# One transfer per query or key tile, bias tables kept on chip, and a moved logarithm in a two-layer attention trunk

## The chip, the cores and the metric

The kernel runs on one core of a Trainium2 chip. A core has TensorE (PE; its weight loads are shown as PEld), VectorE (DVE), ScalarE (ACT), GpSimd (POOL) and SyncE (SP), and 16 DMA engines that move data between the chip's memory (HBM, "DRAM" in the code) and the on-chip memory (SBUF). Nearly all transfers here are issued by SP, in the order of its own instruction queue. The metric is device microseconds of one execution, less is better.

## The reference, cut to what matters

The input is 2,048 tokens of 1,024 floats. Layer 0 has two attention mixers beside each other, layer 1 has one; each layer ends with a SiLU gate, an output projection and a residual add.

```python
# layer 0, mixer A: 8 query heads, 2 key heads, a window of own chunk and 2 before (chunks of 64), a learned sink
probs = softmax(concat([scores, sink]))[..., :-1]
# layer 0, mixer B: 8 heads, own chunk and 8 before, a learned bias by clipped distance
rel = clip(qpos[:, None] - kpos[None, :], -128, 128) + 128
scores = scores + rel_table[:, rel]
# layer 1: 8 heads, each with two maps (q1, k1) and (q2, k2) over all chunks up to the own one
a = softmax(s1) - lam * softmax(s2)
o = rms_norm(a @ v, subln_g) * (1.0 - lambda_init)      # the "sub-norm", per head
x = x + (o * silu(gate)) @ w_out
```

Queries and keys are RMS-normed per head (64 wide) before the scores; mixer A and layer 1 rotate them.

## The kernel before, in words

All arithmetic is in float32, with TensorE working on a high part (H, rounded to the matrix format) and a low part (L, the rest): one product is three or two matmuls. Each layer has a projection stage and a mixing stage. What the projection computes (queries, keys, values, gates) goes through scratch tensors in DRAM and is loaded again, tile by tile, by the mixing stage. Tokens go in 4 blocks of 512 (`BLK`), a block being 4 tiles of 128 (`P`).

*Scratch.* `scratch` (L103) makes one tensor per part: `akH`, `akL` (128 x 2048, two heads of 64 rows each), `bkH`, `bkL` for mixer B, and `qH`, `qL`, `kH`, `kL` (8 heads x 128 rows x 2048) for layer 1. The 128 rows of a layer 1 head are its two maps of 64 rows. `pairs_out` (L384) transposes normed queries or keys, splits them into `eH` and `eL` (three buffers each) and stores each with one transfer (L398, L399).

*Layer 0's mixing* (`_mix0`, L553). For every block from the last to the first, 16 heads alternate in pairs between A and B. `load_q` (L572) fills a query tile of 128 partitions in which the 64 rows of the head stand twice: two transfers for the high part (L577, L578) and two for the low part (L580, L581). `load_k` (L584) fills a key tile with high rows in partitions 0 to 63 and low rows in 64 to 127, again in two transfers (L587, L588). One matmul with the doubled queries then gives high x (high + low). For mixer B each head of each block also loads a bias table of 128 x 256 (L732), turns it round on POOL (L733) and sets a masked corner (L734). Query tiles have three buffers, key tiles, values and bias tables two.

`pace` (L49) lays out the order by hand: the heads' scores come first, the values of a head follow at a lag, and a side stream (late gates, then output projections of finished blocks) is put in between by the share of work done. The output weights' loads are a list; `next_load` (L838) takes one off it after each head (L859) and within the late gates (L866). The framework then orders the instructions of each engine by its own timing model, unless `tc.issue_after(x)` says that what follows is queued behind x on its engine.

*Layer 1's mixing* (`_mix1`, L893). The first two blocks are taken head by head, blocks 2 and 3 after that. `load_q` (L919) fills a tile of 128 partitions x 2 maps x 512 columns: for each part two transfers, one for each half of the partitions, each of 64 rows x 2 maps. `load_k` (L1088) fills a 128 x 512 key tile of one map in two transfers (L1093, L1094); for map 1 the low part stands in the lower half of the partitions. Key tiles have four buffers for each map, query tiles two. `scores` (L929) does the matmuls, a maximum on DVE (L955) and the exponential on ACT (L958), and remembers the newest one in `self.exp`. `gate` (L1030) is called when a head's values are done; its inner `rest` (L1042), called two key tiles into the next head's values, sums squares on PE (L1045), takes the logarithm on ACT (L1046), and goes on with an exponential and a product.

SBUF places are given pool by pool, in the order in which the pools are opened; the mixing stage's pools lie where the projection's pools lay and wait for what is still in use there.

Of the kernel before, what the change touches and what calls it, by code (L numbers as in the profile page):

```python
# [86 lines left out]
class Trunk:  # L87
# [15 lines left out]
    def scratch(self):  # L103
        dram = self.ctx.enter_context(self.tc.tile_pool(name="scr", bufs=1, space=DRAM))

        def d(name, shape):
            return dram.tile(shape, F32, tag=name, name=name)

        self.s0 = {
            "aqH": d("aqH", [4, P, S]), "aqL": d("aqL", [4, P, S]),  # L110
            "akH": d("akH", [1, P, S]), "akL": d("akL", [1, P, S]),
            "av": d("av", [S, 2 * 192]),
            "bqH": d("bqH", [4, P, S]), "bqL": d("bqL", [4, P, S]),
            "bkH": d("bkH", [4, P, S]), "bkL": d("bkL", [4, P, S]),
# [5 lines left out]
            "qH": d("qH", [8, P, S]), "qL": d("qL", [8, P, S]),  # L120
            "kH": d("kH", [8, P, S]), "kL": d("kL", [8, P, S]),
# [102 lines left out]
    def _project(self, es, layer):  # L224
# [15 lines left out]
        xp = pool("x", 3)  # L240
# [143 lines left out]
        def pairs_out(xs, npair, b, o):  # L384
            for p in range(npair):
# [12 lines left out]
                nc.sync.dma_start(s[o["dH"]][o["p0"] + p, :, b * BLK:(b + 1) * BLK], f32(eH))  # L398
                nc.sync.dma_start(s[o["dL"]][o["p0"] + p, :, b * BLK:(b + 1) * BLK], f32(eL))  # L399
# [153 lines left out]
    def _mix0(self, es):  # L553
# [3 lines left out]
        sm = pool("sm", 6)  # L557
        ld = pool("ld", 2)
        sb = pool("sb", 2)
# [12 lines left out]
        def load_q(H, L, h, b, res):  # L572
# [4 lines left out]
            nc.sync.dma_start(f32(qd[0:HD, :]), s[H][h // 2, r, tok])  # L577
            nc.sync.dma_start(f32(qd[HD:P, :]), s[H][h // 2, r, tok])  # L578
            ql = ld.tile([P, BLK], F32R, tag="ql", name=n + "ql", bufs=3)
            nc.sync.dma_start(f32(ql[0:HD, :]), s[L][h // 2, r, tok])  # L580
            nc.sync.dma_start(f32(ql[HD:P, :]), s[L][h // 2, r, tok])  # L581
            res["q"] = (qd, ql)

        def load_k(ks, H, L, p, row, k0, k1):  # L584

            r = slice(row * HD, (row + 1) * HD)
            nc.sync.dma_start(f32(ks[0:HD, :k1 - k0]), s[H][p, r, k0:k1])  # L587
            nc.sync.dma_start(f32(ks[HD:P, :k1 - k0]), s[L][p, r, k0:k1])  # L588
            return ks


        edge = ld.tile([P, 384], F32, tag="edge", name=n + "edge", bufs=1)
# [3 lines left out]
        win = ld.tile([P, 256], F32, tag="win", name=n + "win", bufs=1)  # L596
# [3 lines left out]
        nc.sync.dma_start(far, a["relfar"].to_broadcast([P, 8]))  # L600
        group = {}

        def load_group(b, g):
# [3 lines left out]
            load_k(ks, "akH", "akL", 0, g, k0, k1)  # L607
            vt = ld.tile([P, 5, 192], F32R, tag="vA", name=n + "vA", bufs=1)
# [19 lines left out]
        def join(yt, O, e):  # L628
            hi = slice(e * HD, (e + 1) * HD)
            lo = slice((1 - e) * HD, (2 - e) * HD)  # L630
            tmp = sb.tile([P, BLK], F32, tag="low", name=n + "low", bufs=1)
# [3 lines left out]
        def finish(yt, row, b):  # L635
            gt = ld.tile([P, BLK], F32, tag="gt", name=n + "gt", bufs=1)
# [201 lines left out]
        def next_load(upto=1):  # L838
            if loads and loads[0][0] <= upto:
                _, dst, src = loads.pop(0)  # L840
                nc.sync.dma_start(f32(dst), src)
                return True
# [521 lines left out]
```

## Time and profile before

| | us |
|---|---|
| median of three timed runs | 2790.53 (2790.26 to 2792.29) |
| the profiled execution, its own time | 2787.34 |
| its span, first to last instruction | 2785.4 |
| layer 0's projection, about | 0 to 601 |
| layer 0's mixing, about | 601 to 1126 |
| layer 1's projection, about | 1126 to 1734 |
| layer 1's mixing, about | 1734 to 2785 |

The profile is of one execution. Each engine has a busy time; the waits are named as "waiting instruction <- what released it: total, times, longest". The DMA view has one row for each group of transfers: destination and source, issuing queue, count, KB each, and the median time from issue to landing. The page says "packets" for the pieces that one DMA engine moves at a time: a row of a tile, mostly 2 KB. The granted clock of TensorE was 0.992 on average.

### The profile page before, as it was taken

Reading aid. Unit: us, or ns where it says so; the run is one execution under the profiler, and the core shown is the slowest. Engines: PE = TensorE matmul, PEld = TensorE weight load, DVE = VectorE, ACT = ScalarE, POOL = GpSimd, SP = SyncE. Lnnn points to the kernel's source line nnn. Section 1 sums busy time; section 2 is a strip of 40 time slices with the busy share of each in tenths; the row PEclk is TensorE's granted clock in tenths of the full one; section 3 lists DMA queues with packets and bytes.
Section 4 is the critical chain, followed back from the end, with each engine's and each line's share of the span. In section 5 each row is a group of like instructions: output and inputs, shape, how many; then the busy total and the mean of one; then the engine's idle time right before and its main releaser. Section 6 shows DMA issues by size and latency. Waiting matters only on the chain.

```text
span 2785.4 us, 43642 instructions
## 1 busy us (share of the span) xinstructions
PE 2687.8 (96%) x13384; PEld 2164.0 (78%) x13384; DVE 1814.8 (65%) x4520; ACT 1596.8 (57%) x3975; POOL 1425.9 (51%) x1519
## 2 busy tenths in 40 slices
PE   7999999999899999999999999999999999999999
PEld 6888887888788888788888888777777776676776
DVE  8662286336678776457844783478887787776772
ACT  5443544357777776333243332588887776676771
POOL 3641255235545454325554552467776666667661
PEclk9999999999999999999999999999999999999999
DMA  5674338739777665654386446899877666455542
GB/s 184 213 240 149 110 129 275 239 116 248 221 200 202 192 188 154 200 212 142 130 269 222 131 134 194 250 247 249 213 219 207 198 182 195 125 176 150 165 130 91
DMA packets 354041, 521.64 MB, mean 187 GB/s; under 512 B 42768, under 2 KB 137744, under 8 KB 353808
## 3 DMA queue, kind: packets, MB, share of 16 engines
q1 hardware_dynamic: 349200, 510.47, 61.0%
q10 hardware_dynamic: 4608, 8.39, 0.8%
q8 instruction: 107, 1.75, 0.3%
q14 instruction: 126, 1.03, 0.1%
HBM read 361.70 MB, written 157.02 MB: 186 GB/s over the span
## 4 chain that ended last, share of the span: by engine, by line
PE 68%; DMA 6%; DVE 3%; ACT 3%; issue 2%; POOL 1%; SPq 1%; ACTq 0%; DVEq 0%; POOLq 0%
PE cO L1010 8%; PE p1mm L216 6%; PE p1mm L215 6%; PE p1mm L214 6%; PE cS L951 4%; PE cS L952 4%; PE ctr L1006 4%; PE mom L214 2%; PE mom L215 2%; PE mom L216 2%; PE com L214 2%; PE cG L214 2%; PE com L215 2%; PE cG L215 2%; PE com L216 2%; PE cG L216 2%
## 5 line engine op out<-in xcount | busy, mean ns | idle before, releaser
L958 ACT ACTIVATE cP<-cS,cnm 128x512 f32<-128x512 f32 (+3 forms) x640 | 394.6, 623 | 137.9 <-DVE cnm L955 126.4
L955 DVE TENSOR_REDUCE cnm<-cS 128x1 f32<-128x512 f32 (+3 forms) x640 | 373.4, 600 | 53.8 <-PE cS L952 47.6
L992 POOL TENSOR_TENSOR cP<-cP,cP 128x512 f32<-128x512 f32 (+1 forms) x320 | 356.2, 1140 | 19.2 <-ACT cP L990 18.6
L991 POOL TENSOR_SCALAR cP<-cP,crl,cel 128x512 f32<-128x512 f32 (+3 forms) x288 | 208.8, 737 | 258.4 <-DVE crl L973 111.8
L216 PE MATMUL p1mm<-p1wH,p1hL 128*128 128x512 f32 x768 | 300.5, 392 | 0.0
L214 PE MATMUL p1mm<-p1wH,p1hH 128*128 128x512 f32 x768 | 300.2, 393 | 0.0
L215 PE MATMUL p1mm<-p1wL,p1hH 128*128 128x512 f32 x768 | 299.4, 390 | 0.0
L309 POOL TENSOR_TENSOR p0wL<-p0ws,p0wH 128x512 fp32r<-128x512 f32 (+1 forms) x140 | 169.9, 1240 | 251.0 <-ACT p0wH L307 232.4
L1010 PE MATMUL cO<-cpt,cv 128*128 128x512 f32 (+3 forms) x640 | 286.9, 534 | 5.6 <-DVE cpt L1008 5.6
L951 PE MATMUL cS<-ck,cqd 128*128 128x512 f32 (+3 forms) x640 | 260.6, 411 | 12.5 <-ACT cP L958 11.1
L1008 DVE COPY cpt<-ctr 128x512 f32<-128x512 f32 (+1 forms) x320 | 190.6, 604 | 101.0 <-PE ctr L1006 98.1
L214 PE MATMUL p0mm<-p0wH,p0hH 128*128 128x512 f32 (+1 forms) x640 | 239.1, 377 | 7.4 <-ACT p0vt L497 5.4
L216 PE MATMUL p0mm<-p0wH,p0hL 128*128 128x512 f32 (+1 forms) x640 | 239.3, 374 | 1.3 <-DVE p0hL L335 1.3
L215 PE MATMUL p0mm<-p0wL,p0hH 128*128 128x512 f32 (+1 forms) x640 | 239.5, 374 | 0.0
L952 PE MATMUL cS<-ck,cql 128*128 128x512 f32 (+3 forms) x640 | 233.1, 369 | 1.7 <-DMA cql<-qL 1.7
L1006 PEld LDWEIGHTS ctr<-ident,cP 128*128 128x128 f32 x1088 | 137.3, 141 | 120.0 <-issue 62.6
L309 POOL TENSOR_TENSOR p1wL<-p1ws,p1wH 128x512 fp32r<-128x512 f32 x112 | 154.3, 1402 | 138.8 <-ACT p1wH L307 80.6
L990 ACT ACTIVATE cP<-cP,cc 128x512 f32<-128x512 f32 (+1 forms) x320 | 188.9, 653 | 20.6 <-DVE cc L976 19.6
L1006 PE MATMUL ctr<-ident,cP 128*128 128x128 f32 x1088 | 174.8, 274 | 5.7 <-POOL cP L992 5.7
L216 PEld LDWEIGHTS p1mm<-p1wH,p1hL 128*128 128x128 f32 x768 | 144.2, 188 | 29.4
L215 PEld LDWEIGHTS p1mm<-p1wL,p1hH 128*128 128x128 f32 x768 | 144.3, 188 | 29.0
L214 PEld LDWEIGHTS p1mm<-p1wH,p1hH 128*128 128x128 f32 x768 | 144.3, 188 | 28.5
(320 smaller groups left out, 6937.3 us busy)
## 6 DMA issues: line engine op xcount, KB each, us to landing
p1ws<-in_od_w_in_dram SPq DMA_DIRECT2D x56, 512.0 KB, 3.7
p0ws<-in_ev_w_in_dram SPq DMA_DIRECT2D x48, 512.0 KB, 4.5
ck<-kH SPq DMA_DIRECT2D x144, 128.0 KB, 3.6
ck<-kL SPq DMA_DIRECT2D x144, 128.0 KB, 3.8
cv<-v SPq DMA_DIRECT2D x72, 256.0 KB, 4.4
cqd<-qH SPq DMA_DIRECT2D x64, 256.0 KB, 6.2
cql<-qL SPq DMA_DIRECT2D x64, 256.0 KB, 7.6
cwH<-wgH SPq DMA_DIRECT2D x64, 256.0 KB, 5.3
```

The lines of the kernel that those rows point to most:

```text
L214: mm(ps, aH, bH, start=first, stop=False)
L215: mm(ps, aH, bL, start=False, stop=False)
L216: mm(ps, aL, bH, start=False, stop=last)
L309: low.tensor_tensor(l[:, :width], ws[:, k, :width], f32(h[:, :width]), ALU.subtract)
L951: mm(ps, qd[:, m, js], kt[:, :wd], start=True, stop=False)
L952: self.anchor = mm(ps, ql[:, m, js], kt[:, :wd], start=False, stop=True).ins
L955: nc.vector.tensor_reduce(nm[:, m, z:z + 1], ps, AX.X, ALU.max, negate=True)
L958: exp = nc.scalar.activation(chunks[z][:, :wd], ps, AF.Exp, bias=nm[:, m, z:z + 1], accum_out=acc).ins
L991: nc.gpsimd.tensor_scalar(p1, p1, rl[:, 0:1], e1, ALU.mult, ALU.mult)
L992: nc.gpsimd.tensor_tensor(p1, p1, p2, ALU.add)
L1006: nc.tensor.transpose(turned[:, (j - j0) * P:(j - j0 + 1) * P], us[j][kt // 4][:, kk:kk + P], self.ident)
L1010: mm(O[:, j0 * P:], v, T[:, :wd], start=(kt == 0), stop=(kt == nkt - 1), skip_group_check=True)
```

## The change

- Scratch: high and low keys stand in one tensor (`ak`, `bk`, `ck`), one after the other. Layer 1's queries are laid out by head, row, block, map and column, so that a row's two maps for a block lie together.
- A key tile is loaded by one transfer in both layers, with high rows always in the upper half. A query tile's part is loaded by one transfer whose source is repeated twice. Layer 1's query store writes the two maps in the new order.
- All eight bias tables are loaded once at the start of layer 0's mixing, into a tile of their own, and turned round at their first use, in the last block.
- Pools are opened in another order and some tiles move to pools of their own; layer 1's projection gets four input buffers where it had three.
- Output weights of layer 0 are issued behind the newest query load, and are also taken off their list at every other step of an output tile.
- The sub-norm's logarithm is queued behind the newest exponential.

```diff
+        ak, bk, ck = d("ak", [1, 2, P, S]), d("bk", [4, 2, P, S]), d("ck", [8, 2, P, S])
...
-            "akH": d("akH", [1, P, S]), "akL": d("akL", [1, P, S]),
+            "ak": ak, "akH": ak[:, 0], "akL": ak[:, 1],
...
-            "bkH": d("bkH", [4, P, S]), "bkL": d("bkL", [4, P, S]),
+            "bk": bk, "bkH": bk[:, 0], "bkL": bk[:, 1],
...
-            "qH": d("qH", [8, P, S]), "qL": d("qL", [8, P, S]),
-            "kH": d("kH", [8, P, S]), "kL": d("kL", [8, P, S]),
+            "qH": d("qH", [8, HD, NB, 2, BLK]), "qL": d("qL", [8, HD, NB, 2, BLK]),
+            "k": ck, "kH": ck[:, 0], "kL": ck[:, 1],
@@ _project
-        xp = pool("x", 3)
+        xp = pool("x", 3 + layer)
@@ pairs_out
-                nc.sync.dma_start(s[o["dH"]][o["p0"] + p, :, b * BLK:(b + 1) * BLK], f32(eH))
-                nc.sync.dma_start(s[o["dL"]][o["p0"] + p, :, b * BLK:(b + 1) * BLK], f32(eL))
+                for part, t in (o["dH"], eH), (o["dL"], eL):
+                    to = s[part][o["p0"] + p]
+                    by_map = layer == 1 and o["tab"] == "q"
+                    to = to[:, b].rearrange("r m t -> m r t") if by_map else to[:, b * BLK:(b + 1) * BLK]
+                    nc.sync.dma_start(to, f32(t))
@@ _mix0
         sm = pool("sm", 6)
+        ep = pool("ep", 1)
+        sb = pool("sb", 2)
+        pa = pool("pa", 2)
+        lv = pool("lv", 2)
+        mk = pool("mk", 1)
         ld = pool("ld", 2)
-        sb = pool("sb", 2)
@@ load_q, load_k
-            nc.sync.dma_start(f32(qd[0:HD, :]), s[H][h // 2, r, tok])
-            nc.sync.dma_start(f32(qd[HD:P, :]), s[H][h // 2, r, tok])
             ql = ld.tile([P, BLK], F32R, tag="ql", name=n + "ql", bufs=3)
-            nc.sync.dma_start(f32(ql[0:HD, :]), s[L][h // 2, r, tok])
-            nc.sync.dma_start(f32(ql[HD:P, :]), s[L][h // 2, r, tok])
+            for q, part in (qd, H), (ql, L):
+                self.asked = nc.sync.dma_start(f32(q), s[part][h // 2, r, tok].unsqueeze(0).to_broadcast([2, HD, BLK])).ins
...
-        def load_k(ks, H, L, p, row, k0, k1):
+        def load_k(ks, K, p, row, k0, k1):
...
-            nc.sync.dma_start(f32(ks[0:HD, :k1 - k0]), s[H][p, r, k0:k1])
-            nc.sync.dma_start(f32(ks[HD:P, :k1 - k0]), s[L][p, r, k0:k1])
+            nc.sync.dma_start(f32(ks[:, :k1 - k0]), s[K][p, :, r, k0:k1])
@@ bias tables
+        biases = ld.tile([P, 8, 256], F32, tag="bias", name=n + "bias", bufs=1)
+        for h in range(8):
+            nc.sync.dma_start(biases[:, h, :], a["relb"][h])
...
-            bias = ld.tile([P, 256], F32, tag="bias", name=n + "bias")
-            nc.sync.dma_start(bias, a["relb"][h])
-            nc.gpsimd.tensor_scalar(bias, bias, -1.0, far[:, h:h + 1], ALU.mult, ALU.add)
-            nc.gpsimd.memset(bias[0:HD, 192:256], POS)
+            bias = biases[:, h, :]
+            if b == NB - 1:
+                nc.gpsimd.tensor_scalar(bias, bias, -1.0, far[:, h:h + 1], ALU.mult, ALU.add)
+                nc.gpsimd.memset(bias[0:HD, 192:256], POS)
@@ projected (layer 0)
-                yield from self.out_tile(
+                for i, u in enumerate(self.out_tile(
...
-                )
+                )):
+                    if i % 2:
+                        next_load()
+                    yield u
@@ next_load
-                nc.sync.dma_start(f32(dst), src)
+                with tc.issue_after(self.asked):
+                    nc.sync.dma_start(f32(dst), src)
@@ _mix1: load_q
-                both = s[part][h, :, tok].rearrange("(m r) t -> r m t", m=2)
-                for o in range(2):
-                    nc.sync.dma_start(f32(q[o * HD:(o + 1) * HD]), both)
+                both = s[part][h, :, b].rearrange("r m t -> r (m t)")
+                nc.sync.dma_start(f32(q).rearrange("p m t -> p (m t)"), both.unsqueeze(0).to_broadcast([2, HD, 2 * BLK]))
@@ gate, rest
-                nc.scalar.activation(sq, ms, AF.Ln, bias=self.eps, scale=1.0 / P)
+                with tc.issue_after(self.exp):
+                    nc.scalar.activation(sq, ms, AF.Ln, bias=self.eps, scale=1.0 / P)
@@ _mix1: load_k
-            r, o = slice(m * HD, (m + 1) * HD), slice((1 - m) * HD, (2 - m) * HD)
-            nc.sync.dma_start(f32(k[r, :]), s["kH"][h, r, tok])
-            self.loaded = nc.sync.dma_start(f32(k[o, :]), s["kL"][h, r, tok]).ins
+            self.loaded = nc.sync.dma_start(f32(k), s["k"][h, :, m * HD:(m + 1) * HD, tok]).ins
```

The lines left out rename pools: `low`, `gt`, `sg` move to `ep`; `edge`, `win` to `mk`; `vA`, `v` to `lv`; `PA` to `pa`; calls of `load_k` name the joint tensor.

More of the change, by code (lines that the diff above doesn't have):

```diff
@@ L595, in _mix0 @@
         nc.gpsimd.memset(edge[HD:P, 0:64], POS)
-        win = ld.tile([P, 256], F32, tag="win", name=n + "win", bufs=1)
+        win = mk.tile([P, 256], F32, tag="win", name=n + "win")
         nc.gpsimd.memset(win, 0.0)
@@ L606, in load_group @@
             ks = ld.tile([P, 640], F32R, tag="ksA", name=n + "ksA", bufs=1)
-            load_k(ks, "akH", "akL", 0, g, k0, k1)
-            vt = ld.tile([P, 5, 192], F32R, tag="vA", name=n + "vA", bufs=1)
+            load_k(ks, "ak", 0, g, k0, k1)
+            vt = lv.tile([P, 5, 192], F32R, tag="vA", name=n + "vA", bufs=1)
             nc.sync.dma_start(
@@ L630, in join @@
             lo = slice((1 - e) * HD, (2 - e) * HD)
-            tmp = sb.tile([P, BLK], F32, tag="low", name=n + "low", bufs=1)
+            tmp = ep.tile([P, BLK], F32, tag="low", name=n + "low")
             nc.scalar.activation(tmp[hi, :], O[lo, :], AF.Copy)
@@ L635, in finish @@
         def finish(yt, row, b):
-            gt = ld.tile([P, BLK], F32, tag="gt", name=n + "gt", bufs=1)
+            gt = ep.tile([P, BLK], F32, tag="gt", name=n + "gt")
             nc.sync.dma_start(gt, s["g"][row:row + P, b * BLK:(b + 1) * BLK])
@@ L654, in scores_a @@
             nm, l, es_, r = small("anm", 4), small("al", 4), small("aes", 4), small("ar", 4)
-            pt = sb.tile([P, NTB, 256], F32, tag="PA", name=n + "PA")
+            pt = pa.tile([P, NTB, 256], F32, tag="PA", name=n + "PA")
             lows = [P if b * NTB + j == 0 else 0 for j in range(NTB)]
@@ L724, in scores_b @@
             load_q("bqH", "bqL", h, b, res)
-            ks = load_k(ld.tile([P, 1024], F32R, tag="ks", name=n + "ks"), "bkH", "bkL", h // 2, h % 2, k0, k1)
-            vt = ld.tile([P, 8, P], F32R, tag="v", name=n + "vB")
+            ks = load_k(ld.tile([P, 1024], F32R, tag="ks", name=n + "ks"), "bk", h // 2, h % 2, k0, k1)
+            vt = lv.tile([P, 8, P], F32R, tag="v", name=n + "vB")
             nc.sync.dma_start(
@@ L818, in late_gate @@
                 yield 1
-            sg = sb.tile([P, BLK], F32, tag="sg", name=n + "sg", bufs=1)
+            sg = ep.tile([P, BLK], F32, tag="sg", name=n + "sg")
             gt = yp.tile([P, BLK], F32, tag="xr", name=n + "gt", bufs=2)
@@ L919, in load_q @@
         def load_q(h, b):
-            tok = slice(b * BLK, (b + 1) * BLK)
             qd = ld.tile([P, 2, BLK], F32R, tag="qd", name=n + "qd")
```

2 lines of the change are left out of this document (1 added, 1 removed).

## Prediction

> **What bounds the kernel now.** I read the page's first part first, then the busy time by stage, then the waits of PE on a transfer, then the DMA view of the whole run and of single stretches. All times are microseconds.
>
> ```profile
> span 2785.4 us, 43642 instructions
> PE 2687.8 (96%) x13384; PEld 2164.0 (78%) x13384; DVE 1814.8 (65%) x4520; ACT 1596.8 (57%) x3975; POOL 1425.9 (51%) x1519
> DMA packets 354041, 521.64 MB, mean 187 GB/s; under 512 B 42768, under 2 KB 137744, under 8 KB 353808
> ```
>
> TensorE is the bound: 97.6 us of the span are idle, and no other engine is above 65%. The first two rows below are the end of layer 0's projection, in which the first loads of layer 0's attention are already issued, and layer 1's projection. Then come the three stretches that matter here: layer 0's attention (from its first query load at 533 to its last loads at 1078), a stretch of layer 1's projection in which queries are stored, and layer 1's attention (1690 to 2661). Columns: time, length, five busy times with counts, granted clock, share of the 16 DMA engines, GB/s.
>
> ```profile
> 533.00:601.00 68.00, 68.00 (x301) 56.31 (x300) 8.80 (x13) 23.36 (x38) 16.09 (x20) 1.00 0.53 168
> ...
> 1126.00:1690.00 564.00, 561.27 (x2654) 467.90 (x2653) 359.86 (x597) 205.41 (x419) 275.47 (x207) 1.00 0.55 180
> ```
>
> ```profile
> 533.00:1078.00 545.00, 517.72 (x3138) 450.54 (x3137) 363.67 (x1216) 372.74 (x971) 254.62 (x383) 0.99 0.71 199
> 1690.00:2661.00 971.00, 940.73 (x4294) 696.57 (x4293) 703.63 (x1851) 705.64 (x1856) 615.30 (x660) 0.99 0.70 199
> ```
>
> ```profile
> 1254.00:1348.00 94.00, 94.00 (x449) 78.48 (x447) 74.03 (x120) 31.14 (x65) 53.37 (x40) 1.00 0.41 135
> ```
>
> In both attention stages the DMA engines are busy for seven tenths of the time on average, and PE still hardly waits for them. This is all of PE's idle time that ends with a query load:
>
> ```profile
> PE mSB L619 <- DMA mql<-bqL: 2.5, 4, 1.0
> PE mSA L619 <- DMA mql<-aqL: 2.4, 1, 2.4
> PE cS L952 <- DMA cql<-qL: 1.7, 2, 1.4
> PE cS L951 <- DMA cqd<-qH: 0.6, 1, 0.6
> ```
>
> 7.2 us, and no row names a key load. So what the change can win is small; what it can lose is the cover that the transfers have now, and that hangs on how many engines one transfer runs on.
>
> **How a transfer is divided now.** A quiet stretch shows it: from 300 to 320 only four gate tiles of 128 rows of 2 KB are stored.
>
> ```profile
> DMA packets 576, 1.05 MB, mean 52 GB/s; under 512 B 64, under 2 KB 64, under 8 KB 576
> q1 hardware_dynamic: 576, 1.05, 13.9%
> g<-p0gt SPq DMA_DIRECT2D x4, 256.0 KB, 2.4
> ```
>
> 512 packets are the rows; 64 small ones are left, sixteen for each transfer, one for each engine. 1.05 MB in 13.9% of 16 engines' 20 us is 23.6 GB/s for one engine. The same holds everywhere: the DMA view's 100 groups of issues, of which the first is p1ws x56, hold 2,057 transfers, and 2,057 x 16 = 32,912. The other 9,856 of the page's 42,768 small packets are the data rows under 512 B: cosines and sines 8,192, norms and lambdas 1,024, sinks and far bias 256, three gain columns 384. Even 256 bytes in 64 rows go to sixteen engines:
>
> ```profile
> p1ws<-in_od_w_in_dram SPq DMA_DIRECT2D x56, 512.0 KB, 3.7
> bq_g<-in_ev_b_q_norm_dram SPq DMA_DIRECT2D x2, 0.2 KB, 6.0
> ```
>
> So the division does not go by bytes. What all 2,057 share is an outermost loop over 64 or 128 rows. The change makes transfers with another outermost loop: a query load repeats its source twice (loop 2, zero step, over 64 rows), a key load takes high and low part (loop 2) over 64 rows, and layer 1's query store writes map by map (loop 2) over 64 rows. No row of before has an outermost loop of two. I bound such a transfer by sixteen engines (every row) and by two (one for each turn of the loop). I take two: rows of the outermost loop are the one unit that all transfers here have in common, and two turns give nothing to the other fourteen engines.
>
> The Trainium skill has a rule that speaks against this change. "DMA: Bandwidth & Descriptors", section "Rules for kernel authors", says that the engine count follows from the slowest loop of both sides, and that a leading zero-step broadcast of c copies holds the whole transfer to at most c engines. By it the sum is the one worked out below for two engines; the trace agrees in so far as loops of 64 and 128 run on sixteen, and it has no case of two.
>
> **The change, part by part.** These rows carry the bytes (KB each is 1,024 bytes; MB below is 10^6):
>
> ```profile
> mqd<-aqH SPq DMA_DIRECT2D x64, 128.0 KB, 4.2
> mql<-aqL SPq DMA_DIRECT2D x64, 128.0 KB, 4.5
> mqd<-bqH SPq DMA_DIRECT2D x64, 128.0 KB, 4.5
> mql<-bqL SPq DMA_DIRECT2D x64, 128.0 KB, 5.0
> mks<-bkH SPq DMA_DIRECT2D x24, 256.0 KB, 5.7
> mks<-bkL SPq DMA_DIRECT2D x24, 256.0 KB, 6.2
> mks<-bkH SPq DMA_DIRECT2D x8, 128.0 KB, 3.8
> mks<-bkL SPq DMA_DIRECT2D x8, 128.0 KB, 3.9
> mksA<-akH SPq DMA_DIRECT2D x6, 160.0 KB, 4.3
> mksA<-akL SPq DMA_DIRECT2D x6, 160.0 KB, 4.0
> ck<-kH SPq DMA_DIRECT2D x144, 128.0 KB, 3.6
> ck<-kL SPq DMA_DIRECT2D x144, 128.0 KB, 3.8
> cqd<-qH SPq DMA_DIRECT2D x64, 256.0 KB, 6.2
> cql<-qL SPq DMA_DIRECT2D x64, 256.0 KB, 7.6
> qH<-p1eH SPq DMA_DIRECT2D x32, 256.0 KB, 2.8
> qL<-p1eL SPq DMA_DIRECT2D x32, 256.0 KB, 3.2
> mbias<-in_relb_dram SPq DMA_DIRECT2D x32, 128.0 KB, 5.7
> ```
>
> And these what each of the three stretches moves in all, in the order 533 to 1078, 1254 to 1348, 1690 to 2661 (SP's queue, then ACT's queue in the last):
>
> ```profile
> q1 hardware_dynamic: 82669, 107.60, 70.4%
> ```
>
> ```profile
> q1 hardware_dynamic: 6784, 12.59, 41.0%
> ```
>
> ```profile
> q1 hardware_dynamic: 132632, 189.99, 68.9%
> q10 hardware_dynamic: 1152, 2.10, 0.6%
> ```
>
> The rate of one of the two engines is unknown: 23.6 GB/s from the quiet stretch above; 107.60 MB in 70.4% of 16 x 545 us is 17.5, and 189.99 MB in 68.9% of 16 x 971 is 17.7, when all sixteen pull at once. I take 22, near the quiet row, because fourteen engines would be nearly idle. Transfers on sixteen engines are issued on the same queue and close only when the two loaded engines have moved their rows too, so each stage needs the two engines' confined bytes plus one sixteenth of the rest.
>
> - *Layer 0's attention.* Queries 256 x 131,072 bytes = 33.6 MB, keys 12.6 + 2.1 + 2.0 = 16.7 MB, together 50.2. On two engines that is 25.1 MB each. The rest of the stage stays on sixteen: 107.6 less 50.2 less 24 bias tables (3.1) is 54.3, or 3.4 for each engine. 28.5 MB at 22 GB/s are 1,295 us where the stage has 545: **+750**.
> - *Layer 1's attention.* Queries 128 x 262,144 = 33.6 MB, keys 288 x 131,072 = 37.7; 71.3 MB make 35.65 for each of the two. The rest, 192.1 less 71.3, is 7.55 for each engine. 43.2 MB are 1,964 us instead of 971: **+993**. The cover is used up: PE has 940.73 us of work in this stage, so the transfers end last.
> - *Layer 1's query stores.* In the stretch of 94 us (the other half of the projection has one more, taken as equal) 32 stores of 262,144 bytes are 8.4 MB, 4.2 for each of two engines, and the rest of its 12.59 MB gives 0.26. 4.45 MB are 202 us. The three buffers of each part let six stores (36 us) trail; 202 - 94 - 36 = 72 stall the transposes that fill them, twice: **+144**.
> - *Bias tables.* 24 loads go; so do 24 of the rows below, off PE's path, and the 172.3 us of waiting cost no one but POOL, which works 254.62 of 545 us there. The eight loads now come in front of the first queries, behind 68 us in which PE still has layer 0's projection. 0.
>
> ```profile
> L733 POOL TENSOR_SCALAR mbias<-mbias,mfar 128x256 f32<-128x256 f32 x32 | 15.3, 479 | 172.3 <-DMA mbias<-in_relb_dram 172.3
> L1046 ACT ACTIVATE csq<-cms,eps 128x512 f32<-128x512 f32 x32 | 22.0, 687 | 46.8 <-PE cms L1045 46.8
> ```
>
> - *The sub-norm's logarithm* (L1046) keeps its 687 ns. Behind the newest exponential the 46.8 us that ACT stood at it can go to exponentials instead. Queued behind it are the exponential L1048 and the two-step output for the projection; that consumer runs a whole head later. Between -2 and +2; with ACT at 705.64 of 971 us, 0.
> - *Issue order and places.* Output weights are asked for behind the newest query load, the projection gets a fourth input tile, and pools lie elsewhere. PE's 561 of 564 us in that projection leave nothing to win. What they could cost is the second rival. 0.
>
> Sum: 750 + 993 + 144 = 1,887 us. The profiled execution took 2787.34 us (2 more than its span; 3.2 below the median of the three timed runs, which is about the 0.2%, 5.6 us, that a measurement can tell): 2,787 + 1,887 = **4,675 us** with two engines.
>
> **The rivals.** *All sixteen engines.* If the split reaches the 64 rows below the loop of two, each pair of loads becomes one and nothing is confined. Then the 7.2 us of query waits can go, nothing else on PE's path does: 2,780 us, faster by 0.26%. For it speaks that every transfer of before used sixteen; against it, that each had sixteen or more outermost rows. The Trainium skill's page named above, in the same section, advises one transfer of 128 partitions instead of two of disjoint halves; by that rule this rival's time is the result.
>
> *Sixteen engines and a late start.* Eight bias loads and the reordered places have to wait for memory of the projection; the first head's queries, behind them in SP's order, then come late. It decides once they are later than the 68 us that PE still works after 533. A table and a layer 0 query landing one after the other (5.7 + 5.0 us by their rows) leave PE idle for 10.7: 2,798 us, slower by 0.4%.
>
> *Only the repeated source is confined.* If zero-step loops are held to two engines but high and low parts are not, layer 0 has 33.6/2 + (107.6 - 33.6 - 3.1)/16 = 21.2 MB, 965 us (+420), layer 1 has 16.8 + 158.5/16 = 26.7 MB, 1,213 us (+242), and the stores cost nothing: 3,450 us.
>
> **How the numbers follow.** Two engines 0.83, sixteen 0.12, sixteen with a late start 0.02, only the repeated source 0.03. The weight of the first rests on the count of closing packets, which is blind to bytes, and on the loop of two that no transfer here has; the 0.12 on the possibility that the split sees through it. Within the first case, 23.6 GB/s gives +663, +860 and +124, 4,434 us; since that row is four transfers long I open it to 25 GB/s, 595 + 757 + 106, 4,245. The loaded rates give +1,084, +1,463 and +230, 5,564. The range 4,240 to 5,600 holds all but a few hundredths of the first case, 0.8 in all; what is left out are the three others. Faster: two thirds of the sixteen-engine case, 0.08; within 0.2%: 0.04; slower: 0.88.
>
> **What would show it.** If right, the small packets fall from 42,768 to 30,208 (848 transfers with 16 each go; 440 with two and eight bias loads with 16 come); at sixteen engines they would be 36,368. The mean share of the DMA engines drops in both attention stages while PE idles there, at about 57% of the span, with cqd, cql, ck, mqd, mql and mks as its releasers, and the granted clock falls in many slices; landing of these loads goes from 4 to 8 us to well above 10. The p1eH and p1eL copies wait for their stores. Wrong would be: landings under 8 us with PE still at 96% (sixteen engines), waits only for query loads (third rival), or PE idle at 533 to 620 alone (second).

## The result and the profile after

The changed kernel took 4579.18 us (median of five runs, 4575.36 to 4583.04) where the kernel before took 2792.29 beside it: ratio 1.6413, with a 95% interval of 1.6382 to 1.6443. It is 1,787 us slower. The forecast was 4,675.

The page of the changed kernel, the lines that answer to those shown of before, with the granted clock in 40 slices, SP's queue, and the chain that ended last by engine:

```profile
span 4574.7 us, 43129 instructions
PE 2998.7 (66%) x13384; PEld 2364.4 (52%) x13384; DVE 1810.2 (40%) x4520; ACT 1604.8 (35%) x3975; POOL 1404.5 (31%) x1471
PEclk9999976777777779978987877777777877788779
DMA packets 330214, 518.41 MB, mean 113 GB/s; under 512 B 30209, under 2 KB 122113, under 8 KB 329985
q1 hardware_dynamic: 325376, 507.27, 33.1%
DMA 47%; PE 29%; SPq 6%; DVE 3%; issue 3%; POOL 2%; ACT 1%; POOLq 0%; ACTq 0%; DVEq 0%
```

The granted clock and the chain of the kernel before:

```profile
PEclk9999999999999999999999999999999999999999
PE 68%; DMA 6%; DVE 3%; ACT 3%; issue 2%; POOL 1%; SPq 1%; ACTq 0%; DVEq 0%; POOLq 0%
```

Read the fourth line of the changed kernel first. 30,209 small packets: the prediction's count for two engines was 30,208, that for sixteen 36,368. The bytes are nearly what they were (518 MB against 522), the rate fell from 187 to 113 GB/s, and nearly half of the chain is DMA, which had 6% of it. PE's busy time grew by 311 us for the same 13,384 matmuls while the granted clock fell in most slices (mean 0.812, before 0.992); the other 1,478 us of the longer span are idle time of PE.

The waits of PE, the largest rows that end with a transfer (total, times, longest):

```profile
PE cS L962 <- DMA ck<-ck: 297.3, 64, 14.9
PE mSB L627 <- DMA mqd<-bqH: 166.9, 19, 16.1
PE mSB L628 <- DMA mql<-bqL: 130.4, 29, 6.0
PE cG L216 <- DMA cwH<-wgH: 119.3, 10, 20.5
PE cS L962 <- DMA cqd<-qH: 109.5, 7, 24.0
PE cS L963 <- DMA cql<-qL: 93.2, 10, 13.7
```

Five of the six are tiles that the change loads in one transfer. The sixth, cwH, is a gate weight whose transfer the change does not touch (3.0 us before): what is divided over sixteen engines is late too.

Where the time lies: three matmul groups of before, then of after, with the first and the last start (us) in the second half of each row. mSA and mtrB belong to layer 0's mixing, cS to the scores of layer 1.

```profile
L618 PE MATMUL mSA<-mksA,mqd x128: 219/283/386, 602.6 to 1074.2; 128*128 128x256 f32 x120, 128*128 128x128 f32 x8
L775 PE MATMUL mtrB<-ident,mPB x560: 270/273/435, 620.4 to 1116.5; 128*128 128x128 f32 x187
L951 PE MATMUL cS<-ck,cqd x640: 220/395/799, 1734.4 to 2706.5; 128*128 128x512 f32 x136, 128*128 128x128 f32 x8, 128*128 128x384 f32 x8, 128*128 128x256 f32 x8
```

```profile
L627 PE MATMUL mSA<-mksA,mqd x128: 220/415/582, 615.0 to 1710.0; 128*128 128x256 f32 x120, 128*128 128x128 f32 x8
L784 PE MATMUL mtrB<-ident,mPB x560: 270/273/436, 664.9 to 1778.0; 128*128 128x128 f32 x187
L962 PE MATMUL cS<-ck,cqd x640: 220/443/1041, 2618.4 to 4495.8; 128*128 128x512 f32 x136, 128*128 128x128 f32 x8, 128*128 128x384 f32 x8, 128*128 128x256 f32 x8
```

Up to the last mtrB after is 661.5 us later (1778.0 - 1116.5), from there to the first cS it loses 222.5 (840.4 instead of 617.9), between the first and the last cS 905.3 (1877.4 instead of 972.1), and behind that nothing (78.9 in both). Together 1,789, the whole difference of the spans. The forecast's terms for these parts were 750, 144 and 993.

The same by stage, in columns as in the prediction's rows (time, length, five busy times, clock, share of 16 engines, GB/s): layer 0's attention, one stretch of query stores, layer 1's attention.

```profile
533.00:1714.00 1181.00, 636.99 (x3120) 540.54 (x3118) 364.49 (x1213) 376.76 (x972) 239.52 (x337) 0.74 0.26 88
1912.00:2096.00 184.00, 110.40 (x451) 88.38 (x450) 74.56 (x122) 29.45 (x67) 51.97 (x40) 0.80 0.19 65
2574.00:4450.00 1876.00, 1064.98 (x4216) 762.64 (x4214) 695.20 (x1840) 718.26 (x1858) 619.41 (x665) 0.76 0.31 103
```

The share of the DMA engines fell from about 0.7 to 0.26 and 0.31 in the attention stages, although transfers now end last. That is how a few loaded engines look in a mean over sixteen. A stretch of 20 us in which queries are stored shows it bare, first by the DMA view, then by SP's timeline (start, length, instruction); the last fence is the start of the same stores, 112 us earlier:

```profile
DMA packets 508, 1.02 MB, mean 51 GB/s; under 512 B 8, under 2 KB 8, under 8 KB 508
q1 hardware_dynamic: 508, 1.02, 13.1%
```

```profile
2024.97 4.96 SPq L404 DMA_DIRECT2D qL<-p1eL  x1
2030.03 4.95 SPq L404 DMA_DIRECT2D qH<-p1eH  x1
2035.07 4.96 SPq L404 DMA_DIRECT2D qL<-p1eL  x1
2040.12 4.91 SPq L303 DMA_DIRECT2D p1ws<-in_od_w_in_dram  x1
```

```profile
1912.06 1.13 SPq L404 DMA_DIRECT2D qH<-p1eH  x2
1913.28 8.80 SPq L404 DMA_DIRECT2D qL<-p1eL  x2
```

13.1% of 16 is 2.1 engines (two packets are under way for 18 of the 20 us and three for the other 2); the four stores of the stretch closed with eight small packets, two each. The first two stores are handed over in 1.13 us together. After them each issue begins about 5 us behind the one before and lasts nearly as long: SP waits for room. That the room comes free as the two engines take a store in is inferred from these times. 131,072 bytes per engine in the 4.95 us of an issue are 26.5 GB/s, the rate that the sums below use; by the 5.05 us from one issue to the next it is 26.0. The weight load p1ws, which is divided over sixteen engines, stands in the same line.

### The profile page after: what moved, and what is told of

The parts are those of the page before. It is cut to its first block, busy times and chain, and to the rows that moved or that the text cites. A ratio compares the mean times of both kernels' runs of the same rounds, so it can differ in the third digit from the quotient of the medians.

```text
span 4574.7 us, 43129 instructions
## 1 busy us (share of the span) xinstructions
PE 2998.7 (66%) x13384; PEld 2364.4 (52%) x13384; DVE 1810.2 (40%) x4520; ACT 1604.8 (35%) x3975; POOL 1404.5 (31%) x1471
## 2 busy tenths in 40 slices
DMA packets 330214, 518.41 MB, mean 113 GB/s; under 512 B 30209, under 2 KB 122113, under 8 KB 329985
## 4 chain that ended last, share of the span: by engine, by line
DMA 47%; PE 29%; SPq 6%; DVE 3%; issue 3%; POOL 2%; ACT 1%; POOLq 0%; ACTq 0%; DVEq 0%
DMA ck<-ck 10%; DMA mql<-bqL 9%; DMA cql<-qL 5%; DMA cwH<-wgH 5%; DMA mql<-aqL 4%; PE cO L1021 4%; DMA qL<-p1eL 3%; PE cS L962 2%; DMA p1ws<-in_od_w_in_dram 2%; PE cS L963 2%; PE p1mm L218 2%; PE p1mm L216 2%; PE p1mm L217 2%; PE ctr L1017 2%; DMA x<-mxr 1%
## 5 line engine op out<-in xcount | busy, mean ns | idle before, releaser
L962 PE MATMUL cS<-ck,cqd 128*128 128x512 f32 (+3 forms) x640 | 293.2, 461 | 435.5 <-DMA ck<-ck 297.3
L962 PEld LDWEIGHTS cS<-ck,cqd 128*128 128x128 f32 x640 | 136.8, 214 | 493.9 <-issue 418.9
L217 PE MATMUL p1mm<-p1wL,p1hH 128*128 128x512 f32 x768 | 311.3, 405 | 47.1 <-POOL p1wL L311 47.0
L216 PE MATMUL p1mm<-p1wH,p1hH 128*128 128x512 f32 x768 | 312.3, 409 | 45.0 <-DVE p1xn L371 29.4
L963 PE MATMUL cS<-ck,cql 128*128 128x512 f32 (+3 forms) x640 | 260.3, 408 | 93.2 <-DMA cql<-qL 93.2
L218 PE MATMUL p1mm<-p1wH,p1hL 128*128 128x512 f32 x768 | 311.4, 406 | 0.0
L1021 PE MATMUL cO<-cpt,cv 128*128 128x512 f32 (+3 forms) x640 | 306.5, 567 | 0.6 <-DVE cpt L1019 0.5
L1017 PEld LDWEIGHTS ctr<-ident,cP 128*128 128x128 f32 x1088 | 147.0, 149 | 125.8 <-issue 70.7
L627 PE MATMUL mSB<-mks,mqd 128*128 128x384 f32 (+2 forms) x240 | 95.1, 397 | 177.9 <-DMA mqd<-bqH 166.9
L963 PEld LDWEIGHTS cS<-ck,cql 128*128 128x128 f32 x640 | 139.5, 218 | 114.2 <-DMA cql<-qL 96.7
```

The lines of the kernel that those rows point to most:

```text
L216: mm(ps, aH, bH, start=first, stop=False)
L217: mm(ps, aH, bL, start=False, stop=False)
L218: mm(ps, aL, bH, start=False, stop=last)
L962: mm(ps, qd[:, m, js], kt[:, :wd], start=True, stop=False)
L963: self.anchor = mm(ps, ql[:, m, js], kt[:, :wd], start=False, stop=True).ins
L1017: nc.tensor.transpose(turned[:, (j - j0) * P:(j - j0 + 1) * P], us[j][kt // 4][:, kk:kk + P], self.ident)
```

## The experiments

The theory: the outermost loop of a transfer sets how many engines it runs on, and the two loaded engines end last. Single runs stand beside 2789.17 (first four kernels), 2800.73 (next four) or 2788.15 (last four) of the kernel before on the same chip; 2800.73 is itself a single run, so differences from it are good to some 10 us.

**Rows outermost, and two transfers again.** If the loop order is the cause, the change loses nothing once each transfer has 64 or 128 rows outermost. The first kernel swaps the loops of every query and key load (rows then stand interleaved in partitions, in queries and keys alike, so the scores are the same); the second keeps everything else of the change but loads halves. Both send each of layer 1's query stores out as two transfers of 64 rows.

```diff
-  s[part][h // 2, r, tok].unsqueeze(0).to_broadcast([2, HD, BLK])
+  s[part][h // 2, r, tok].unsqueeze(1).to_broadcast([HD, 2, BLK])
...
-  nc.sync.dma_start(f32(ks[:, :k1 - k0]), s[K][p, :, r, k0:k1])
+  nc.sync.dma_start(f32(ks[:, :k1 - k0]), s[K][p, :, r, k0:k1].rearrange("i r t -> r i t"))
...
-  to = to[:, b].rearrange("r m t -> m r t") if by_map else to[:, b * BLK:(b + 1) * BLK]
-  nc.sync.dma_start(to, f32(t))
+  if by_map:
+      for m in range(2):
+          nc.sync.dma_start(to[:, b, m], f32(t[m * HD:(m + 1) * HD, :]))
```

> The changed kernel with one thing turned round: in every query and key load the loop over 64 rows is outermost and the loop of two (the repeat, or high and low part) is inside it, so that the row r stands in partitions 2r and 2r+1 of both tiles; the number of loads and their bytes stay. The query stores of layer 1, which cannot be turned, go out as two of 64 rows each. Theory (a transfer runs on as many engines as its outermost loop feeds, two in the changed kernel): all sixteen engines again, 2,770 to 2,795 us, PE busy about 96%, small packets 42,768 - 13,568 + 504 x 16 + 128 = 37,392. Rival one (a repeated source, a joint tensor or rows of 4 KB is slow as such): nothing changes but the stores, 4,350 to 4,600 us. Rival two (the stall comes from the bias loads, the places or the issue order): the same 4,350 to 4,600 us with the transfers quick and PE waiting for other things.

The second kernel loads each query and key tile in two transfers of 64 rows:

```diff
-  self.asked = nc.sync.dma_start(f32(q), s[part][h // 2, r, tok].unsqueeze(0).to_broadcast([2, HD, BLK])).ins
+  for o in range(2):
+      self.asked = nc.sync.dma_start(f32(q[o * HD:(o + 1) * HD, :]), s[part][h // 2, r, tok]).ins
```

> The changed kernel with every query and key tile loaded by two transfers of 64 rows, as before the change, and layer 1's query stores as two of 64 rows; bias tables on chip, places, issue order, the moved logarithm and the new layouts stay. Theory: 2,770 to 2,800 us. Against the kernel of before this is the worth of all parts but the single transfers, against the kernel with the row loop outermost it is the worth of the single transfers by themselves: I expect at most 10 us between the two, for a transfer less costs SP about half a microsecond that PE does not wait for. Rival two (the rest of the change makes the stall): over 4,000 us.

Measured: 2778.25 us with rows outermost (ratio to before 0.996, 0.9941 to 0.9979) and 2776.51 with two transfers (0.9954, 0.9939 to 0.997). The whole 1,787 us are gone in both. The page with rows outermost:

```profile
span 2772.8 us, 43210 instructions
DMA packets 337398, 518.44 MB, mean 187 GB/s; under 512 B 37392, under 2 KB 129296, under 8 KB 337168
```

The loads are as few as in the change and the bytes are the same; the closing packets rose from 30,209 to 37,392, sixteen for each transfer again. The outermost loop of two is the whole loss. That bias tables, places and issue order came along unchanged in both kernels clears them as well.

**Layer 1's keys alone.** The kernel before with one edit:

```diff
-  nc.sync.dma_start(f32(k[r, :]), s["kH"][h, r, tok])
-  self.loaded = nc.sync.dma_start(f32(k[o, :]), s["kL"][h, r, tok]).ins
+  self.loaded = nc.sync.dma_start(f32(k), s["k"][h, :, m * HD:(m + 1) * HD, tok]).ins
```

> The kernel of before with one part of the change: layer 1's key tiles come in one transfer whose outermost loop is of two. Theory: 37.75 MB on two engines is 18.9 each, the rest of the stage gives 154.3/16 = 9.6; 28.5 MB at the 26.5 GB/s that the changed kernel's back-to-back query stores show (131,072 bytes in 4.95 us) are 1,076 us where the stage has 971, and the two engines stood idle for a tenth of the time there, so 1,200: about 3,000 us (2,890 to 3,100), small packets 42,768 - 288 x 16 + 144 x 2 = 38,448. Rival (joint high and low parts are not confined, only a repeated source is): 2,780 to 2,795 us and 40,464 packets.

Measured: 3302.45 us, 513 more than before. That two engines carry it is right (38,448 small packets), so a loop over high and low part is confined just as a repeated source is, and the third rival of the prediction is out. The size missed: 513 where about 210 were expected.

**The query stores alone.** The new layout and the store map by map, with loads of two times 64 rows:

```diff
+  to = to[:, b].rearrange("r m t -> m r t") if by_map else to[:, b * BLK:(b + 1) * BLK]
+  nc.sync.dma_start(to, f32(t))
```

> The kernel of before with one part of the change: layer 1's queries in the new layout, each part stored by one transfer whose outermost loop is the two maps; loads stay two of 64 rows for each part. Theory: the two stretches of query stores take 184 us each as in the changed kernel, not 94: 2,787 + 180 = about 2,970 us (2,930 to 3,020), nothing lost in the attention stages. Rival (stores are not confined): 2,780 to 2,800 us.

Measured: 2994.98 us, 206 more than before, and 41,872 small packets. From this kernel's waits, four rows of one chain, then the wait that I had foreseen; below them the first row as it was before:

```profile
ACT p1wH L307 <- DMA p1ws<-in_od_w_in_dram: 140.3, 25, 21.3
POOL p1wL L309 <- ACT p1wH L307: 141.7, 25, 18.3
PE p1mm L215 <- POOL p1wL L309: 47.4, 6, 13.5
PE p1trq L388 <- POOL p1xn L381: 81.0, 10, 15.7
DVE p1eL L394 <- DMA qL<-p1eL: 151.6, 16, 14.2
```

```profile
ACT p1wH L307 <- DMA p1ws<-in_od_w_in_dram: 69.1, 27, 6.1
```

The copies do wait for their stores. But the projection's weights wait too: their loads are queued behind the stores on SP, and PE stands until they are split. PE's largest wait, 81.0 us that it did not have before, belongs to the same chain, as at 1297 us: POOL makes the normed queries p1xn in the order of its queue, and it stood 18.3 us before a weight split that comes ahead of them.

**Four turns instead of two.** The keys missed by so much that the count of engines had to be tested by itself. Keys are laid out in four groups of 32 rows, and the outermost loop has four turns:

```diff
+  ck = d("ck", [8, 2, 4, 33, S])
...
-  nc.sync.dma_start(f32(k[r, :]), s["kH"][h, r, tok])
-  self.loaded = nc.sync.dma_start(f32(k[o, :]), s["kL"][h, r, tok]).ins
+  self.loaded = nc.sync.dma_start(f32(k), s["k"][h, m, :, 0:32, tok]).ins
```

> The kernel before with layer 1's keys loaded in one transfer per tile whose outermost loop counts four (four groups of 32 rows, high and low) where the keys-alone kernel had two; each part of a key pair is stored in four transfers of 32 rows. Outermost loop sets the number of engines (my theory): four engines, 37.75 MB / 4 + 154.3 MB / 16 = 19.1 MB for each of them, 720 us at 26.5 GB/s where the stage has 971; the stage is nearly what it was, and the whole 2,790 to 2,900, the upper end for 192 more store issues in the projection. Rival (any loop outside the rows that is not itself the rows drops to the same slow path, whatever its count): about 3,300, as with two.

Measured: 3039.46 us, between the two. The page of this kernel:

```profile
DMA packets 353082, 521.65 MB, mean 172 GB/s; under 512 B 41808, under 2 KB 136784, under 8 KB 352848
```

42,768 - 288 x 16 + 144 x 4 + 192 x 16 = 41,808: four closing packets for each key load, sixteen for each of the 192 additional stores. Four turns run on four engines and cost 239 where two cost 513; the additional stores are in the 239. PE's wait for a key load, with two turns and then with four:

```profile
PE cS L953 <- DMA ck<-ck: 271.8, 59, 10.5
```

```profile
PE cS L959 <- DMA ck<-ck: 90.2, 33, 6.9
```

So the count matters and isn't a switch between one slow and one quick path. The loss was still far above what I expected for four.

**More key buffers.** One guess for the missing size was a ring: a key buffer comes free late, and its next tile then takes 5 us. Six buffers for each map, with room taken from the spare hidden tiles, and key loads that may run two tiles further ahead:

```diff
-  kp = pool("kp", 4)
+  kp = pool("kp", 6)
...
-  hx = pool("hx", 3)
+  hx = pool("hx", 1)
...
-  after, spare = [None, {}], NB - keys(b)
+  after, spare = [None, {}], NB + 2 - keys(b)
```

> The kernel before with layer 1's keys in one transfer of two outermost turns, as in the keys-alone kernel (3,302), but six key buffers for each map in place of four; room for them comes from two of three spare hidden tiles. Theory of a ring (two engines are only about 73% busy in that kernel's stage because a buffer comes free late and its next tile takes 5 us or more): 3,150 or less. Rival (the two engines' rate in this stage is simply lower, about 19 GB/s with the other traffic): unchanged, 3,260 to 3,320.

Measured: 3264.58 us, 38 less than with four buffers (one run each, on different chips), not the 150 that the ring asked for. PE's largest waits in this kernel:

```profile
PE com L216 <- DVE cxr L1184: 108.5, 5, 40.4
PE cG L216 <- DMA cwH<-wgH: 83.9, 10, 23.7
PE cS L953 <- DMA ck<-ck: 69.1, 10, 13.1
```

The wait for keys fell from 271.8 to 69.1 and came back at gate weights and at the residual (cxr), whose transfers are divided over sixteen engines. The ring is out as the main cause, and a throughput as what ends last fits: whoever asks next waits for it. What the two spare hidden tiles that were given up cost by themselves no run tells.

**Queries alone, and layer 0's keys alone.** Three kernels, each the kernel before with one group of loads in one transfer of two turns:

```diff
+  nc.sync.dma_start(f32(q), s[part][h // 2, r, tok].unsqueeze(0).to_broadcast([2, HD, BLK]))
```

> The kernel before with only layer 0's query parts loaded in one transfer, the source repeated twice outermost. My theory, two engines: 16.8 MB + 74.0 / 16 = 21.4 MB for each of the two, 808 us at 26.5 GB/s where the stage has 545: 3,050, and up to 3,130 if the two idle a fifth of the time. Rival (transfers one after the other, the two engines 73% busy as in the keys-alone kernel's stage): 1,107 us, 3,350. If a repeated source were not confined: 2,790.

```diff
+  nc.sync.dma_start(f32(q).rearrange("p m t -> p (m t)"), both.unsqueeze(0).to_broadcast([2, HD, 2 * BLK]))
```

> The kernel before with only layer 1's query parts loaded in one transfer, the source repeated twice outermost, and stored as two transfers of 64 rows in the new order. Two engines: 16.8 MB + 158.5 / 16 = 26.7 MB for each, 1,007 us at 26.5 GB/s where the stage has 971: 2,830, and up to 2,940 if keys queued behind a 10 us query transfer come late. Rival (73% busy): 1,380 us, 3,200.

```diff
+  nc.sync.dma_start(f32(ks[:, :k1 - k0]), s[K][p, :, r, k0:k1])
```

> The kernel before with only layer 0's key tiles loaded in one transfer of two outermost turns. If confined and divided transfers take turns (confined bytes at 26.5 GB/s on two engines, then the rest at 17.6 on sixteen, as the runs so far fit): 16.7 / 2 = 8.35 MB, 315 us, plus 90.9 / 16 = 5.7 MB, 323 us, and some 70 idle, 710 us where the stage has 545: 2,950. Rival (both kinds run beside each other and the two engines pull 26.5 GB/s throughout): 14.0 MB, 530 us, at most 2,840.

Measured: 3210.54 (+410), 3145.09 (+344) and 2967.59 (+179). The first two missed upward, as the keys had. The third was expected by another sum, 2,950, and came within 18.

That sum comes from the records of the DMA packets: for each moment of a stage, how many packets are under way. The number is near that of the engines at work, not the same: packets of one engine can overlap (before has up to 26 under way on sixteen engines, and the quiet stretch above three for a tenth of its time on two). Time in us by that number; the stretches are before's 533 to 1078 and 1690 to 2661, moved and lengthened by the shifts of mSA and cS in each kernel:

```
stretch                              0     1-2   3-4   5-8    9+   length
layer 0, before                     79      21    11    48   386      545
layer 0, queries alone              51     479   112    39   273      954
layer 0, keys alone                 49     233    52    64   328      726
layer 0, whole change               41     788   130    37   186    1,181
layer 1, before                    163      28    13    74   693      971
layer 1, keys, two turns           154     551   115    81   575    1,476
layer 1, keys, four turns          170      38   229   159   609    1,205
layer 1, queries alone              82     477    90   118   560    1,327
layer 1, whole change               87   1,095   173   100   420    1,876
```

Two engines work by themselves for most of what a stage has grown by, and with four turns the time moves from the column 1-2 to 3-4. So the two engines need their confined bytes at 26.5 GB/s and on top the time that their share of the divided packets takes now (before: 70.4% of 545 for 107.6 MB, 69.5% of 971 for 192.1 MB); then there is the time in which no engine works. With the column 0 read from each kernel, so that the sum is an account and not a forecast:

```
stretch                       confined/2   at 26.5   rest   none     sum   measured
layer 0, queries alone          16.8 MB       634     264     51     949        954
layer 0, keys alone              8.35         315     324     49     688        726
layer 0, whole change           25.1          947     194     41   1,182      1,181
layer 1, queries alone          16.8          634     557     82   1,273      1,327
layer 1, keys, two turns        18.9          712     543    154   1,409      1,476
layer 1, whole change           35.65       1,345     424     87   1,856      1,876
```

All six lie within about 5%, and still do at 26.0 GB/s. With four turns the same sum gives 356 + 543 + 170 = 1,069 against 1,205; that gap isn't explained. The kernel with six key buffers, counted alike, has 107 us without a packet where four buffers had 154, and 524 with one or two where they had 551: the buffers took idle time away, not the time of the two engines.

**Another issuing queue.** Is it SP's line that holds the divided transfers up? Layer 1's queries alone, issued by ScalarE:

```diff
-  nc.sync.dma_start(f32(q).rearrange("p m t -> p (m t)"), both.unsqueeze(0).to_broadcast([2, HD, 2 * BLK]))
+  nc.scalar.dma_start(f32(q).rearrange("p m t -> p (m t)"), both.unsqueeze(0).to_broadcast([2, HD, 2 * BLK]))
```

> The kernel with only layer 1's query parts in one doubled transfer (3,145), but these transfers issued on ScalarE's queue in place of SyncE's. If SyncE's queue is what makes divided transfers wait (nothing behind a confined transfer is issued while it is being issued), divided transfers now run beside the confined ones: the time in which only one or two DMA engines work falls from 459 us in the attention stage to under 200, and the whole to 2,830 to 3,000; ScalarE, with 705 us of work in a stage of 971, pays for its own issues of 5 to 10 us each. Rival (the DMA engines themselves take the two kinds in turns, whoever issues): 3,100 to 3,200 and the 459 us stay.

Measured: 3193.26 us, no better than from SP (3145.09), and the time with one or two packets under way was 526 us where it had been 477 by the table. In this kernel, an issue row of ScalarE and one of SP (minimum, median, maximum ns) and three waits of PE; below them two of these waits with the queries issued by SP:

```profile
L931 ACTq DMA_DIRECT2D cql<-qL x32: 489/490/9527, 1717.5 to 3008.1; - x32
L1098 SPq DMA_DIRECT2D ck<-kH x144: 444/516/1628, 1694.0 to 3065.5; - x144
PE cS L957 <- DMA cql<-qL: 109.0, 14, 13.5
PE cS L956 <- DMA ck<-kL: 53.2, 21, 8.6
PE cG L214 <- DMA cwH<-wgH: 14.8, 4, 5.3
```

```profile
PE cG L214 <- DMA cwH<-wgH: 95.5, 9, 19.1
PE cS L956 <- DMA ck<-kL: 1.8, 1, 1.8
```

ScalarE's issues mostly took half a microsecond, so it hardly paid. SP was no longer held: its longest issue of a high key part took 1.6 us, where one had taken 11.1 us with the queries on SP. Yet the divided key loads, which no longer stood behind confined ones on SP, were waited for 21 times instead of once; the wait for gate weights fell in turn. So here SP's line decided who waited and not how long the whole took, which leaves the engines themselves as the place where the transfers meet. The Trainium skill says so in "DMA: Bandwidth & Descriptors", section "Issuing engines are not separate DMA queues": whoever issues, transfers run on the same sixteen engines and interleave. The trace agrees.

**The two small edits alone.** The bias tables, then the logarithm, each put into the kernel before:

```diff
+  biases = ld.tile([P, 8, 256], F32, tag="bias", name=n + "bias", bufs=1)
+  for h in range(8):
+      nc.sync.dma_start(biases[:, h, :], a["relb"][h])
```

> The kernel before with only the bias tables loaded once and kept on chip. The change with every loop repaired gained 11 to 13 us (ratio 0.995 to 0.996). If the tables are what gained it: 2,775 to 2,780. My prediction's term for them (nothing): 2,785 to 2,791, ratio within 0.998 to 1.002.

```diff
-  nc.scalar.activation(sq, ms, AF.Ln, bias=self.eps, scale=1.0 / P)
+  with tc.issue_after(self.exp):
+      nc.scalar.activation(sq, ms, AF.Ln, bias=self.eps, scale=1.0 / P)
```

> The kernel before with only the sub-norm's logarithm queued behind the newest exponential. My prediction's term (between -2 and +2 us): ratio 0.999 to 1.001. If this edit is what the repaired change gained: 2,775 to 2,780, ratio 0.995 to 0.996.

Measured: tables 2780.84 us, ratio 0.9971 (0.9955 to 0.9987); logarithm 2791.35, ratio 1.0009 (0.9994 to 1.0025). The tables gain some 7 or 8 us, the logarithm nothing that can be measured. By the middle values the tables are most of the 11 to 13 us that the two repaired kernels gain; the intervals overlap, so that no further gain is shown.

## Why the prediction was right, and where its sizes were off

*Two engines.* Right, and shown: 30,209 closing packets, 2.1 engines busy in the quiet stretch, and the loss gone when only the loops are swapped. The step that carried it was the count of small packets: it told from the profile of before that each transfer closes on sixteen engines whatever its bytes, and so that the loops, not the bytes, decide. The Trainium skill's page "DMA: Bandwidth & Descriptors" agrees in its section "Rules for kernel authors"; the other rule of that section, one transfer of 128 partitions instead of two halves, holds only together with it: with rows outermost one transfer and two take the same time here (ratios 0.996 and 0.9954), with the loop of two outermost it costs 64%.

*The rate of 22 GB/s.* The mis-sized term, in both directions. A confined engine runs faster than I took (26.0 GB/s by SP's spacing of 5.05 us, 26.5 by the length of an issue), the divided bytes fit at the price that they had before (17.5 and 17.7), and the engines also stand idle for some time. Over a whole stage these make 28.5 MB / 1,181 = 24.1 GB/s in layer 0 and 43.2 / 1,876 = 23.0 in layer 1, close to 22; so +750 came out as +661 (with the tail of mtrB) and +993 as +905. That one rate for both kinds comes so close is luck: in the whole change the errors nearly cancel. Taken part by part the single rate is worse: layer 1's keys alone would have been 28.5 / 22 = 1,295 us, measured 1,476. The sum that fits prices the confined bytes and the rest apart. Layer 0's keys also lack two rows, mksA x2 of 128 KB for the high and the low part: 0.5 MB, or some 10 us of the +750 at 22 GB/s, and less than 10 us in the sums above.

*The stores.* +144, measured +206 alone and +222 in the change. The step that failed is the 36 us that six stores were to trail without harm. Bytes at 26.5 GB/s give 4.45 MB / 26.5 = 168 us, and the stretch took 184 (the second one, 2300 to 2484, too): nothing trailed, because the projection's weight loads stand behind the stores and are wanted at once. That +144 came near is again two errors, a rate too low and a trail that isn't there. Two stretches lengthened by 90 us are 180; the other 26 to 42 us lie outside them and I did not follow them.

*Signs that were foreseen.* Waits for cqd, cql, ck, mqd and mql came as named, mks never as a releaser of PE, though mixer A's keys (mksA) were one for 12.2 us. The copies p1eL wait 152.2 us for their stores. PE's share was to be 57% and is 66%: not because it waits less, but because the same matmuls took 311 us longer while the clock fell to 0.812. That this lower clock cost time by itself no run tells. Landing times, which I wanted to see above 10 us, are not given for these groups in the profile after.

*Bias tables at 0.* Off by some 7 or 8 us of gain, ratio 0.9971. Whether POOL's wait of 172.3 us, which I wrote off as nobody's loss, has a part in it isn't shown. One profile differs from another by several us in a stage (the first mSA matmul came at 598.2 with the logarithm alone, at 602.6 before), so where the gain lies stays open.

*Logarithm, order and places at 0.* The logarithm is shown: 0.9994 to 1.0025. For order and places only this is shown: the repaired change with them is not measurably different from the tables alone.

*The rivals.* The sixteen-engine rival's 2,780 is what the repaired kernels take (2778.25 and 2776.51), and the query waits that it struck out are gone in the one with rows outermost. Its condition was false, and that its time came out is partly luck: it priced only the 7.2 us of query waits, but the tables, priced at 0, gain about as much alone, and the kernel with two transfers still has 6.3 us of query waits and is not slower. The late start behind the tables did not occur: the first mSA matmul came at 615.0 instead of 602.6 in the change, but at 625.5 with the queries alone and 619.1 with layer 0's keys alone, which have no tables in front, and at 598.4 with tables in front and rows outermost.

## What to carry to other kernels

Before joining transfers, look at the outermost loop of each side: a joined tile whose outermost loop is a part, a map or a repeated source runs on as many engines as that loop has turns (two and four here, where 64 and 128 rows run on sixteen), and with the loops of the loads swapped nothing was lost (2778.25 us). The count of small closing packets tells on how many engines the transfers run, before and after. Price a confined transfer on its own engines, at their rate alone, on top of what these engines already do for all other transfers, which fitted two turns and was too low for four, and expect divided loads to be late with it, whether SP or ScalarE issues it.

## What the runs showed of the hardware

- *Joined rows cost the engines less.* In layer 1's attention the kernel with rows outermost and the one with two transfers move the same 200 GB/s, the first with a DMA share of 0.61, the second with 0.68. PE was the bound in both, so it shows in no time. Layer 0's attention has 0.64 against 0.70 at 194 GB/s. Why is not shown. The rows of layer 1, in the same columns as above:

```profile
1690.00:2661.00 971.00, 941.57 (x4307) 697.57 (x4306) 712.25 (x1860) 713.74 (x1877) 621.94 (x665) 0.99 0.61 200
```

```profile
1690.00:2661.00 971.00, 939.87 (x4301) 696.17 (x4300) 705.36 (x1852) 712.11 (x1870) 621.30 (x666) 0.99 0.68 200
```

- *An issue can last as long as a transfer takes.* Before, an issue of a key load took 540 ns in the median (at most 1,903); in the change the median is 2,258 ns and the longest 9,800. The row of before, then that of the change (minimum, median, maximum in ns):

```profile
L1093 SPq DMA_DIRECT2D ck<-kH x144: 444/540/1903, 1690.8 to 2661.1; - x144
```

```profile
L1104 SPq DMA_DIRECT2D ck<-ck x144: 479/2258/9800, 2554.6 to 4444.0; - x144
```

- *Confined transfers meet on the same engines.* At 1912 two stores are handed over in 1.13 us, though one takes about 5 us to move, and still two or three packets are under way for nearly all of the time up to 1943. In the change's layer 1 attention one or two packets were under way for 1,095 us and three or four for 173. Different transfers were not put on different pairs. The Trainium skill's page has the rule that such a transfer takes the lowest-numbered engines ("DMA: Bandwidth & Descriptors", section "Why a DMA increments its semaphore by 16 and not by 1"); the trace doesn't number the engines, but its counts fit.
- *The granted clock was lower where PE idled more.* 0.992 before with PE busy for 96% of the span, 0.918 at 84% with layer 1's keys alone, 0.812 at 66% in the change, 0.994 and 0.995 at 97% and 96% with rows outermost and with two transfers. Which of the two brings the other about no run separates.
